# Loading half of the compressed blocks' pages from Pool's queue, with the weights first, and one more step between transposes and state updates

## The chip, the cores and the metric

The kernel runs on one core of a Trainium2 chip. A core has five engines with queues of their own: TensorE (PE: matrix products; PEld is its loading of weights), VectorE (DVE), ScalarE (ACT), GpSimd (POOL) and SyncE (SP), which here only issues transfers. Transfers are issued by SP or by Pool and carried out by 16 DMA engines that both share. The metric is the device time of one execution in microseconds (us); lower is better.

## The reference, cut to what matters

One layer of a hybrid decoder for 1024 prompt tokens and 64 sample tokens (8 sequences of 8 tokens, each with 512 cached tokens in four pages of 128). After one input projection the layer does sparse attention (compressed blocks, selected blocks, sliding window) beside a gated linear recurrence, then a common output projection and an MLP. Two parts matter here.

```
def compress(rows, pe, w1, w2):        # a block of 64 rows -> one compressed key or value
    blk = rows.reshape(b, nc, 64, N_KV_HEADS, 64) + pe
    blk = blk.transpose(...).reshape(b, nc, N_KV_HEADS, 64 * 64)
    return silu(blk @ w1) @ w2         # w1: 4096 x 128, w2: 128 x 64
...
# recurrence, per chunk of 64 tokens and head
S = exp(last) * S + einsum('sd,se->de', k * exp(last - cum), v)
```

`compress` runs over the rows of the prompt and over the cached rows, which lie in 32 pages that a page table names; once for keys (w = 0) and once for values (w = 1).

## The kernel before, in words

The whole layer is one function, `trunk`, written out without loops at run time. Each instruction is put on its engine's queue by a planner: it follows the order in which the Python code issues the instructions as a priority, and takes what its own model of time holds to be ready, so that each queue is a fixed order. A queue is in order: an instruction that waits holds everything behind it.

**Features.** `proj` multiplies the normalised input by 128 columns of the input weights, in three groups of tokens. A group is 24 matmuls (lines 136 to 138, eight blocks of three, since each operand is split in a high and a low half); the generator yields once after 12 of them and once after the evacuation of the group. `weave` alternates such half groups with one step each of a second generator.

**Recurrence.** That second generator is `recurrent`, one for each of four pairs of heads. Its steps are: gate and decay; query; transposes of the weighted keys (L647, L651) and their copies out of PSUM (`k3T`, L648, L649, L652); then, in one step, `swish` of the output gate (L101 on VectorE, L102, L104 and L105 on ScalarE, a product on Pool), the copy of the decay (L657), the first eight state updates (L662) and their copies out of PSUM (L665); a second eight updates; the scan over chunks (L667); attention within a chunk (L678); and so on, to the normalised output in `mix_out`. The updates write the PSUM tile `big`, of which there is one, so the second eight wait for the copies of the first.

**Compression.** After the last pair there is a branch on a flag (L741). Then `compress` issues its loads on SP's queue: 32 pages into the tile `cm` (L263; two runs of 512 bytes in each of 128 partitions, the page number from a register that was read at L732), the position encoding (L267), eight loads of the prompt's rows from `c_d` (L272, runs of 128 bytes), w2 (L275) and three quarters of w1 (L280, 512 KB each, three buffers; the next quarter is loaded when one has been used up). The last two features, 6 and 7, are multiplied while these loads run; then come the 64 products of the compression (L288, two instructions each). From the 45th product on, the first attention scores (`measure`, L843) are put between them. These need the tiles `B1` and `B2`, built by VectorE and ScalarE (L775, L786) from `augk` and `k_d`, which are loaded by SP at L779 and L781; the values (`v_d`, L790) have the same four buffers. The first queries are loaded at L949 and L955 and cast at L958 to L960.

**Pool's queue** before the change: elementwise products, the split of the weights of the recurrent output projection, and ten transfers, among them the writes of `k_d`, `q_d` (L546) and `c_d`, and the mask `dm` (L761).

Of the kernel before, what the change touches and what calls it, by code (L numbers as in the profile page):

```python
# [29 lines left out]
N_PAGES = 32  # L30
POOL_PAGES = 40
# [19 lines left out]
def trunk(ctx: ExitStack, tc: tile.TileContext, I, O):  # L51
# [205 lines left out]
    def compress(ch):  # L257


        mp = pool(ch, "cmp")  # L260
        cm = tl(mp, [128, 2, 161, 32], tag="cm")
        for j in range(N_PAGES):
            S.dma_start(cm[:, :, 4 * j:4 * j + 4].rearrange("p w x s -> p w (x s)"),  # L263
                        I["cache_c"][bass.ds(pages[j], 1)].rearrange("o p (w x) -> (o p) w x", w=2))
            if j % 4 == 3:
                yield -1
        S.dma_start(cm[:, :, 160], I["cmp_pe"])  # L267
        for w in range(2):
            for g in range(2):
                src = c_d[w][g * 64:(g + 1) * 64, :TP].rearrange("d (b h s) -> h d b s", h=2, s=32)  # L270
                for h in range(2):
                    S.dma_start(cm[64 * h:64 * h + 64, w, 128 + g * 16:144 + g * 16], src[h])  # L272
                yield -1
        w2 = tl(mp, [128, 2, 64], tag="w2")
        S.dma_start(w2, I["cmp_w2"])  # L275
        w1 = [[None] * 4 for _ in range(2)]

        def load_w1(w, q):
            w1[w][q] = tl(mp, [128, 8, 128], tag="w1", bufs=3)
            S.dma_start(w1[w][q], I["cmp_w1"][w][:, 8 * q:8 * q + 8])  # L280

        for q in range(3):
            load_w1(0, q)
        yield -2
        for w in range(2):
            ph2 = tl(ps, [128, 512], tag="sc", bufs=SC)
            for s in range(32):
# [59 lines left out]
    with ExitStack() as c:  # L347
# [245 lines left out]
        def recurrent(pr, f, tq, sg):  # L593
# [58 lines left out]
            A.copy(k3T[:64, 8], pt[:64])  # L652
            yield
            swish(sg, tq)

            by_entry = k[:, :TP].rearrange("p (e c) -> p e c", c=16)
            V.tensor_copy(k3[:, :TP].rearrange("p (e c) -> p e c", c=16), decay[:, None, :].to_broadcast([128, 64, 16]))  # L657
            for c0 in range(0, 16, 8):
                pu = tl(ps, [128, 2, 4, 128], tag="big")
                for j in range(8):  # L660
                    ci = c0 + j
                    PE.matmul(pu[:, j % 2, j // 2], k3T[halves[ci % 2], ci // 2], vp[halves[ci % 2], ci // 2],  # L662
                              start=True, stop=True)
                for hs in halves:
                    A.copy(by_entry[hs, :, c0:c0 + 8].rearrange("p e (c u) -> p u c e", u=2), pu[hs, :, :, hs])  # L665
                yield
            V.tensor_tensor_scan(k[:, :TP], k3[:, :TP], k[:, :TP], 0.0, op0=ALU.mult, op1=ALU.add)  # L667
            for hs, copy in zip(halves, (A.copy, V.tensor_copy)):
# [53 lines left out]
        for pr in range(4):  # L722
            f, tq, sg = (tl(hp, [128, T], tag=t) for t in ("tf", "tq", "tg"))
            for j, t in enumerate((f, tq, sg)):
                if j == 2:
                    run(side)
                    side = recurrent(pr, f, tq, sg)
                    next(side)
                weave(scaled(3 * pr + (RF, RQ, RG)[j], t), side if j < 2 else iter(()))
            next(side)  # L730
            if pr == 0:
                pages = [S.value_load(pgt[:1, j:j + 1], min_val=0, max_val=POOL_PAGES - 1) for j in range(N_PAGES)]  # L732
            for i in FEATS[pr]:
                weave(feature(i), side)
        run(side)
# [10 lines left out]
        nl = nlg.rearrange("p t (h r) -> p t r h", r=3)  # L746
        ccp = ExitStack()
        cg = compress(ccp)
        while next(cg) != -2:
            pass  # L750
        for i in FEATS[4]:
            run(feature(i))
        catch_up()
# [22 lines left out]

    for br in range(2):
        ak = tl(bp, [112, TP], tag="b", bufs=4)
        S.dma_start(ak[64:], I["augk"][br])  # L779
        st = tl(bp, [128, TP], tag="b", bufs=4)  # L780
        S.dma_start(st, k_d[br])  # L781
        for g in range(2):
            rows = slice(64 * g, 64 * g + 64)
            for h in range(2):
                bring(B1[64 * h:64 * h + 64, br, g], st[rows])
            V.tensor_tensor(B2[:64, br, g], st[rows], B1[rows, br, g].bitcast(F32), op=ALU.subtract)  # L786
            bring(B2[64:, br, g], ak[64:])
    for t in range(0, 8, 4):
        st = tl(bp, [128, 4, 4, 64], tag="b", bufs=4)
        S.dma_start(st.rearrange("p t b d -> p t (b d)"), v_d[:, t:t + 4])  # L790
        for x in range(4):
            split(st[:, x], VV[:, t + x, :, 0], VV[:, t + x, :, 1])
    cbp.close()
# [343 lines left out]
                          po[64 * g:64 * g + 64].rearrange("p (b c) -> p b c", c=64)[:, :, g * 32 + r * 8:g * 32 + r * 8 + 8])  # L1137
        norm_out(oS, range(4), slice(TP, T), sp, "pt1", 1)

    def out_rnn(rp, groups, other):  # L1140

        units = [(o, n, m) for o, n in groups for m in range(8)]
        stream = ahead([I["w_or"][m] for _, _, m in units], (G,))
# [12 lines left out]
        for u, (o, n, m) in enumerate(units):  # L1156
            wh, wl = next(stream)
            if u == 0:
                yield 0
            if u + 1 < len(units) and units[u + 1][2]:  # L1160
                load(u + 1)
            next(other, None)
            p = tl(ps, [128, 512], tag="mm", bufs=MMB)
            hl = parts[o]
            yield from mm3(p[:, :n], [(wh[:, kc], wl[:, kc], hl[0][:, kc, :n], hl[1][:, kc, :n]) for kc in range(4)])
            if u + 1 < len(units) and not units[u + 1][2]:
                load(u + 1)
            V.tensor_tensor(xs[u][:, :n], xs[u][:, :n], p[:, :n], op=ALU.add)
            S.dma_start(part_d[m][:, o:o + n], xs[u][:, :n])
# [108 lines left out]
    oT0 = H0[:, :4]  # L1278
    rs0 = tl(hp0, [128, n0], tag="rs0")
    crp = ExitStack()  # L1280
    r0 = out_rnn(pool(crp, "outr"), OG, iter(()))
    next(r0)
    attend([(i, g) for g in range(2) for i in range(NQ0)], filler(r0, "outr", "att0", FILL0), oT0, first)

# [214 lines left out]
```

## Time and profile before

| | us |
|---|---|
| median of 3 runs | 1716.74 (1715.77 to 1717.94) |
| the profiled execution's own time | 1714.56 |
| its span in the profile | 1712.8 |

The profile shows one execution. An engine is busy while it works on an instruction; issuing transfers does not count. "<-" in a row of a timeline or of the waits names what ended the idle time before an instruction. The clock (PEclk) is the share of TensorE's full speed that was granted. The DMA share is the mean over 16 engines and can come out above 1.

### The profile page before, as it was taken

Reading aid. Unit: us, or ns where it says so; the run is one execution under the profiler, and the core shown is the slowest. Engines: PE = TensorE matmul, PEld = TensorE weight load, DVE = VectorE, ACT = ScalarE, POOL = GpSimd, SP = SyncE. Lnnn points to the kernel's source line nnn. Section 1 sums busy time; section 2 is a strip of 40 time slices with the busy share of each in tenths; the row PEclk is TensorE's granted clock in tenths of the full one; section 3 lists DMA queues with packets and bytes.
Section 4 is the critical chain, followed back from the end, with each engine's and each line's share of the span. In section 5 each row is a group of like instructions: output and inputs, shape, how many; then the busy total and the mean of one; then the engine's idle time right before and its main releaser. Section 6 shows DMA issues by size and latency. Waiting matters only on the chain.

```text
span 1712.8 us, 25987 instructions
## 1 busy us (share of the span) xinstructions
PE 1636.1 (96%) x9719; PEld 1501.2 (88%) x9741; DVE 947.7 (55%) x1775; ACT 745.3 (44%) x1554; POOL 360.1 (21%) x306
## 2 busy tenths in 40 slices
PE   8999999999599999999999999999999999999999
PEld 6898898988477777788887778999999999999999
DVE  6245655535446778777777756464553352443442
ACT  5334644444336677667766633243421221221211
POOL 0031313211004435333233311010320120120110
PEclk9999999999789999999999999999999999999999
DMA  5333132213934442121211167355322221222222
GB/s 193 121 80 94 54 104 87 65 58 123 247 106 147 138 134 79 40 64 59 70 53 56 53 192 219 115 166 175 108 68 69 74 62 62 81 68 74 62 91 76
DMA packets 135616, 170.84 MB, mean 100 GB/s; under 512 B 37659, under 2 KB 80987, under 8 KB 135483
## 3 DMA queue, kind: packets, MB, share of 16 engines
q1 hardware_dynamic: 134042, 164.38, 31.3%
q0 software_dynamic: 1440, 4.74, 0.9%
q8 instruction: 78, 1.28, 0.3%
q14 instruction: 56, 0.45, 0.1%
HBM read 140.70 MB, written 28.84 MB: 99 GB/s over the span
## 4 chain that ended last, share of the span: by engine, by line
PE 62%; DVE 6%; issue 2%; SPq 2%; ACT 2%; DMA 1%; POOL 0%; DVEq 0%; POOLq 0%; ACTq 0%
PE mm L136 15%; PE mm L137 15%; PE mm L138 15%; PE tr L916 2%; PE O L897 2%; PE O L898 2%; PE sc L843 1%; PE tr L917 1%; PE sc L288 1%; PE sc L844 1%; SPq L263 1%; DVE wl L109 1%; DVE mxs L849 1%; PE sc L1087 1%; PE sc L805 1%
## 5 line engine op out<-in xcount | busy, mean ns | idle before, releaser
L136 PE MATMUL mm<-ah,wh 128*128 128x352 f32 (+1 forms) x736 | 249.1, 338 | 0.0
L136 PE MATMUL mm<-uh,wh 128*128 128x352 f32 (+1 forms) x736 | 244.6, 332 | 0.0
L108 ACT CAST wh<-ws 128x512 fp32r<-128x512 f32 x183 | 105.6, 618 | 313.6 <-PE mm L137 240.0
L137 PE MATMUL mm<-al,wh 128*128 128x352 f32 (+1 forms) x736 | 242.0, 329 | 0.0
L138 PE MATMUL mm<-ah,wl 128*128 128x352 f32 (+1 forms) x736 | 241.4, 328 | 0.0
L138 PE MATMUL mm<-uh,wl 128*128 128x352 f32 (+1 forms) x736 | 240.3, 327 | 0.0
L137 PE MATMUL mm<-ul,wh 128*128 128x352 f32 (+1 forms) x736 | 240.1, 326 | 0.0
L1231 POOL TENSOR_TENSOR sq<-r 128x352 f32<-128x352 f32 (+1 forms) x96 | 99.3, 1034 | 563.4 <-DVE r L1229 553.6
L924 POOL TENSOR_TENSOR pl<-e,ph 128x512 fp32r<-128x512 f32 x88 | 117.8, 1343 | 255.4 <-ACT ph L923 154.0
L136 PE MATMUL mm<-X,wh 128*128 128x364 f32 (+1 forms) x480 | 164.7, 343 | 0.0
L138 PE MATMUL mm<-X,wl 128*128 128x364 f32 (+1 forms) x480 | 160.8, 335 | 3.9 <-PEq L741 3.9
L109 DVE TENSOR_TENSOR wl<-ws,wh 128x512 fp32r<-128x512 f32 x174 | 139.9, 841 | 38.3 <-ACT wh L108 37.8
L137 PE MATMUL mm<-X,wh 128*128 128x364 f32 (+1 forms) x480 | 160.9, 335 | 0.0
L136 PEld LDWEIGHTS mm<-ah,wh 128*128 128x128 f32 x736 | 140.0, 190 | 3.4 <-issue 2.2
L137 PEld LDWEIGHTS mm<-al,wh 128*128 128x128 f32 x736 | 139.5, 190 | 3.9 <-issue 2.7
L136 PEld LDWEIGHTS mm<-uh,wh 128*128 128x128 f32 x736 | 138.9, 189 | 1.9 <-issue 0.8
L138 PEld LDWEIGHTS mm<-uh,wl 128*128 128x128 f32 x736 | 138.2, 188 | 1.5 <-issue 1.2
L137 PEld LDWEIGHTS mm<-ul,wh 128*128 128x128 f32 x736 | 138.4, 188 | 1.1
L138 PEld LDWEIGHTS mm<-ah,wl 128*128 128x128 f32 x736 | 138.9, 189 | 0.5
L1243 DVE TENSOR_TENSOR H<-H,mm 128x352 f32<-128x352 f32 (+1 forms) x92 | 48.8, 530 | 156.2 <-PE mm L138 154.6
L108 ACT CAST wh<-w 128x512 fp32r<-128x512 f32 x153 | 89.5, 616 | 100.3 <-PE mm L137 70.7
L109 DVE TENSOR_TENSOR wl<-w,wh 128x512 fp32r<-128x512 f32 x134 | 115.7, 891 | 28.9 <-ACT wh L108 28.6
(405 smaller groups left out, 3441.3 us busy)
## 6 DMA issues: line engine op xcount, KB each, us to landing
ws<-w_up SPq DMA_DIRECT2D x82, 256.0 KB, 2.8
ws<-w_down SPq DMA_DIRECT2D x80, 256.0 KB, 2.8
w<-w_down SPq DMA_DIRECT2D x48, 256.0 KB, 2.6
w<-w_up SPq DMA_DIRECT2D x46, 256.0 KB, 2.8
w<-w_feat SPq DMA_DIRECT2D x40, 256.0 KB, 2.9
w<-w_or SPq DMA_DIRECT2D x19, 256.0 KB, 2.7
cm<-cache_c SPq DMA_DIRECT2D x32, 128.0 KB, 2.6
w<-cmp_w SPq DMA_DIRECT2D x8, 512.0 KB
```

The source lines that it names most:

```text
L108: A.copy(wh, w)
L109: (eng or V).tensor_tensor(wl, w, wh.bitcast(F32), op=ALU.subtract)
L136: PE.matmul(p, wh, zh, start=i == 0, stop=False)
L137: PE.matmul(p, wh, zl, start=False, stop=False)
L138: PE.matmul(p, wl, zh, start=False, stop=i == n - 1)
L263: S.dma_start(cm[:, :, 4 * j:4 * j + 4].rearrange("p w x s -> p w (x s)"), I["cache_c"][bass.ds(pages[j], 1)].rearrange("o p (w x) -> (o p ...
L897: PE.matmul(po(), vst, ph[:m], start=si == 0, stop=False, skip_group_check=True)
L898: PE.matmul(po(), vst, pl[:m], start=False, stop=end, skip_group_check=True)
L916: PE.matmul(pt, B1[:, br, g, ks], A1, start=True, stop=False)
L924: (G if turn_[0] % 3 < 2 else V).tensor_tensor(pl, e, ph.bitcast(F32), op=ALU.subtract)
L1231: G.tensor_tensor(sq[:, :n], r[:, :n], r[:, :n], op=ALU.mult)
L1243: V.tensor_tensor(H[:, m, sl], H[:, m, sl], p[:, :n], op=ALU.add)
```

## The change: what it does

- `compress`: the first quarter of w1 is issued first. Pages with odd numbers are loaded from Pool's queue, with page numbers that Pool reads itself; pages with even numbers stay on SP. The second quarter comes after the four loads of c_d for the keys, the third after those for the values, and w2 last. The yields between the loads go.
- `recurrent`: one more yield, behind `swish`. Of the two copies of the updated states one goes to VectorE.
- `augk`, `k_d` and `v_d` are loaded from Pool's queue.
- `out_rnn` loses a parameter that was always an empty iterator.

```
@@ -259,29 +259,29 @@

         mp = pool(ch, "cmp")
         cm = tl(mp, [128, 2, 161, 32], tag="cm")
+        w2 = tl(mp, [128, 2, 64], tag="w2")
+        w1 = [[None] * 4 for _ in range(2)]
+
+        def load_w1(w, q):
+            w1[w][q] = tl(mp, [128, 8, 128], tag="w1", bufs=3)
+            S.dma_start(w1[w][q], I["cmp_w1"][w][:, 8 * q:8 * q + 8])
+
+        load_w1(0, 0)
         for j in range(N_PAGES):
-            S.dma_start(cm[:, :, 4 * j:4 * j + 4].rearrange("p w x s -> p w (x s)"),
-                        I["cache_c"][bass.ds(pages[j], 1)].rearrange("o p (w x) -> (o p) w x", w=2))
-            if j % 4 == 3:
-                yield -1
+            eng, page = (G, pages_g[j // 2]) if j % 2 else (S, pages[j])
+            eng.dma_start(cm[:, :, 4 * j:4 * j + 4].rearrange("p w x s -> p w (x s)"),
+                          I["cache_c"][bass.ds(page, 1)].rearrange("o p (w x) -> (o p) w x", w=2))
         S.dma_start(cm[:, :, 160], I["cmp_pe"])
         for w in range(2):
             for g in range(2):
                 src = c_d[w][g * 64:(g + 1) * 64, :TP].rearrange("d (b h s) -> h d b s", h=2, s=32)
                 for h in range(2):
                     S.dma_start(cm[64 * h:64 * h + 64, w, 128 + g * 16:144 + g * 16], src[h])
-                yield -1
-        w2 = tl(mp, [128, 2, 64], tag="w2")
+            if w == 0:
+                load_w1(0, 1)
+        load_w1(0, 2)
         S.dma_start(w2, I["cmp_w2"])
-        w1 = [[None] * 4 for _ in range(2)]
-
-        def load_w1(w, q):
-            w1[w][q] = tl(mp, [128, 8, 128], tag="w1", bufs=3)
-            S.dma_start(w1[w][q], I["cmp_w1"][w][:, 8 * q:8 * q + 8])
-
-        for q in range(3):
-            load_w1(0, q)
-        yield -2
+        yield None
         for w in range(2):
             ph2 = tl(ps, [128, 512], tag="sc", bufs=SC)
             for s in range(32):
@@ -652,6 +652,7 @@
             A.copy(k3T[:64, 8], pt[:64])
             yield
             swish(sg, tq)
+            yield

             by_entry = k[:, :TP].rearrange("p (e c) -> p e c", c=16)
             V.tensor_copy(k3[:, :TP].rearrange("p (e c) -> p e c", c=16), decay[:, None, :].to_broadcast([128, 64, 16]))
@@ -661,8 +662,8 @@
                     ci = c0 + j
                     PE.matmul(pu[:, j % 2, j // 2], k3T[halves[ci % 2], ci // 2], vp[halves[ci % 2], ci // 2],
                               start=True, stop=True)
-                for hs in halves:
-                    A.copy(by_entry[hs, :, c0:c0 + 8].rearrange("p e (c u) -> p u c e", u=2), pu[hs, :, :, hs])
+                for hs, copy in zip(halves, (A.copy, V.tensor_copy)):
+                    copy(by_entry[hs, :, c0:c0 + 8].rearrange("p e (c u) -> p u c e", u=2), pu[hs, :, :, hs])
                 yield
             V.tensor_tensor_scan(k[:, :TP], k3[:, :TP], k[:, :TP], 0.0, op0=ALU.mult, op1=ALU.add)
             for hs, copy in zip(halves, (A.copy, V.tensor_copy)):
@@ -729,7 +730,8 @@
                 weave(scaled(3 * pr + (RF, RQ, RG)[j], t), side if j < 2 else iter(()))
             next(side)
             if pr == 0:
-                pages = [S.value_load(pgt[:1, j:j + 1], min_val=0, max_val=POOL_PAGES - 1) for j in range(N_PAGES)]
+                pages, pages_g = ([eng.value_load(pgt[:1, j:j + 1], min_val=0, max_val=POOL_PAGES - 1) for j in js]
+                                  for eng, js in ((S, range(N_PAGES)), (G, range(1, N_PAGES, 2))))
             for i in FEATS[pr]:
                 weave(feature(i), side)
         run(side)
@@ -746,8 +748,7 @@
         nl = nlg.rearrange("p t (h r) -> p t r h", r=3)
         ccp = ExitStack()
         cg = compress(ccp)
-        while next(cg) != -2:
-            pass
+        next(cg)
         for i in FEATS[4]:
             run(feature(i))
         catch_up()
@@ -776,9 +777,9 @@

     for br in range(2):
         ak = tl(bp, [112, TP], tag="b", bufs=4)
-        S.dma_start(ak[64:], I["augk"][br])
+        G.dma_start(ak[64:], I["augk"][br])
         st = tl(bp, [128, TP], tag="b", bufs=4)
-        S.dma_start(st, k_d[br])
+        G.dma_start(st, k_d[br])
         for g in range(2):
             rows = slice(64 * g, 64 * g + 64)
             for h in range(2):
@@ -787,7 +788,7 @@
             bring(B2[64:, br, g], ak[64:])
     for t in range(0, 8, 4):
         st = tl(bp, [128, 4, 4, 64], tag="b", bufs=4)
-        S.dma_start(st.rearrange("p t b d -> p t (b d)"), v_d[:, t:t + 4])
+        G.dma_start(st.rearrange("p t b d -> p t (b d)"), v_d[:, t:t + 4])
         for x in range(4):
             split(st[:, x], VV[:, t + x, :, 0], VV[:, t + x, :, 1])
     cbp.close()
@@ -1137,7 +1138,7 @@
                           po[64 * g:64 * g + 64].rearrange("p (b c) -> p b c", c=64)[:, :, g * 32 + r * 8:g * 32 + r * 8 + 8])
         norm_out(oS, range(4), slice(TP, T), sp, "pt1", 1)

-    def out_rnn(rp, groups, other):
+    def out_rnn(rp, groups):

         units = [(o, n, m) for o, n in groups for m in range(8)]
         stream = ahead([I["w_or"][m] for _, _, m in units], (G,))
@@ -1159,7 +1160,6 @@
                 yield 0
             if u + 1 < len(units) and units[u + 1][2]:
                 load(u + 1)
-            next(other, None)
             p = tl(ps, [128, 512], tag="mm", bufs=MMB)
             hl = parts[o]
             yield from mm3(p[:, :n], [(wh[:, kc], wl[:, kc], hl[0][:, kc, :n], hl[1][:, kc, :n]) for kc in range(4)])
@@ -1278,7 +1278,7 @@
     oT0 = H0[:, :4]
     rs0 = tl(hp0, [128, n0], tag="rs0")
     crp = ExitStack()
-    r0 = out_rnn(pool(crp, "outr"), OG, iter(()))
+    r0 = out_rnn(pool(crp, "outr"), OG)
     next(r0)
     attend([(i, g) for g in range(2) for i in range(NQ0)], filler(r0, "outr", "att0", FILL0), oT0, first)

```

## Rows read from the trace of the kernel before

**Rows 1.** The page, busy time and share of the span for each engine.
```profile
PE 1636.1 (96%) x9719; PEld 1501.2 (88%) x9741; DVE 947.7 (55%) x1775; ACT 745.3 (44%) x1554; POOL 360.1 (21%) x306
```

**Rows 2.** Waits of TensorE over the span: sum in us, times, longest.
```profile
PE sc L288 <- DMA w<-cmp_w: 18.2, 2, 14.8
PE big L662 <- DVE k3T L649: 8.0, 2, 4.0
PE big L662 <- DVE decay L628: 5.2, 2, 4.0
PE big L662 <- ACT k L665: 1.2, 1, 1.2
```

**Rows 3.** Timeline of TensorE: start and duration in us, instruction, count.
```profile
416.69 0.33 PE L136 MATMUL mm<-X,wh 128*128 128x360 f32 x1
...
420.52 0.33 PE L138 MATMUL mm<-X,wl 128*128 128x360 f32 x1
...
451.35 13.47 PE L288 MATMUL sc<-cm,w 128*128 128x161 f32 x48 [14.78 <-DMA w<-cmp_w]
...
480.46 0.47 PE L843 MATMUL sc<-B,A 128*128 128x128 f32 x1
```

**Rows 4.** Timeline of SP's queue, the loads around the compression.
```profile
410.74 25.73 SPq L263 DMA_DIRECT2D cm<-cache_c  x32
...
437.23 8.56 SPq L272 DMA_DIRECT2D cm<-c_d  x8
...
446.85 1.32 SPq L280 DMA_DIRECT2D w<-cmp_w  x3
...
449.21 0.58 SPq L779 DMA_DIRECT2D b<-augk  x1
...
461.09 0.33 SPq L790 DMA_DIRECT2D b<-v_d  x1
...
463.26 1.92 SPq L280 DMA_DIRECT2D w<-cmp_w  x3
```

**Rows 5.** Busy time by stretch: length, engines, then clock, DMA share, GB/s.
```profile
416.00:436.60 20.60, 19.05 (x111) 18.25 (x110) 10.57 (x20) 10.46 (x22) 3.14 (x3) 1.00 0.66 198
440.00:448.00 8.00, 0.00 (x0) 0.00 (x0) 0.00 (x0) 0.00 (x0) 0.00 (x0) 0.50 1.21 206
```

**Rows 6.** Timeline of pair 1, from the sigmoid to the state copies.
```profile
203.12 1.11 ACT L102 ACTIVATE tq<-tq 128x1088 f32<-128x1088 f32 x1 [4.63 <-DVE tq L101]
...
204.14 0.57 ACT L648 COPY k3T<-big 128x512 f32<-128x512 f32 x1
...
204.74 0.69 DVE L649 COPY k3T<-big 128x512 f32<-128x512 f32 x1 [0.45 <-ACT k3T L648]
...
205.49 2.08 PE L662 MATMUL big<-vp,k3T 64*128 64x128 f32 x16 [3.97 <-DVE decay L628]
...
207.90 2.12 ACT L665 COPY k<-big 64x512 f32<-64x512 f32 x2
```

**Rows 7.** Pool's transfers of q_d: as an instruction, and from issue to landing.
```profile
L546 POOL DMA_DIRECT2D q_d<-nrm x4 | 2.3, 574 | 22.2 <-DVE qS L545 19.5 <-DVE nrm L541 2.7
...
q_d<-nrm POOLq DMA_DIRECT2D x4, 512.0 KB, 4.1
```

**Rows 8.** Timeline of VectorE, the last cast of the first two queries.
```profile
470.78 0.69 DVE L959 TENSOR_TENSOR A<-stage,A 64x512 fp32r<-64x512 f32 x1
```

**Rows 9.** Line 732, the reading of page numbers on SP.
```profile
L732 SPq TENSOR_LOAD <-pgt x32: 262/264/477, 24.2 to 45.8; - x32
```

**Rows 10.** Busy time by stretch behind the updates of pairs 0, 1, 2, 3.
```profile
134.10:141.00 6.90, 5.73 (x52) 5.19 (x53) 2.60 (x2) 5.55 (x8) 2.52 (x1) 1.00 0.01 4
205.50:213.00 7.50, 7.50 (x47) 6.85 (x48) 2.59 (x2) 4.90 (x7) 2.51 (x1) 0.62 0.05 19
278.10:288.00 9.90, 9.81 (x112) 8.95 (x114) 2.14 (x3) 5.73 (x6) 2.50 (x1) 0.83 0.23 70
349.00:357.00 8.00, 8.00 (x51) 7.38 (x52) 0.28 (x1) 4.65 (x6) 2.50 (x1) 0.66 0.03 12
```

More of the change, by code (lines that the diff above doesn't have):

```diff
@@ L261, in compress, with load_w1 @@
         cm = tl(mp, [128, 2, 161, 32], tag="cm")
+        w2 = tl(mp, [128, 2, 64], tag="w2")
+        w1 = [[None] * 4 for _ in range(2)]
+        def load_w1(w, q):
+            w1[w][q] = tl(mp, [128, 8, 128], tag="w1", bufs=3)
+            S.dma_start(w1[w][q], I["cmp_w1"][w][:, 8 * q:8 * q + 8])
+        load_w1(0, 0)
         for j in range(N_PAGES):
[L263 to L266, printed above, removed]
+            eng, page = (G, pages_g[j // 2]) if j % 2 else (S, pages[j])
+            eng.dma_start(cm[:, :, 4 * j:4 * j + 4].rearrange("p w x s -> p w (x s)"),
+                          I["cache_c"][bass.ds(page, 1)].rearrange("o p (w x) -> (o p) w x", w=2))
         S.dma_start(cm[:, :, 160], I["cmp_pe"])
@@ L272, in compress @@
                     S.dma_start(cm[64 * h:64 * h + 64, w, 128 + g * 16:144 + g * 16], src[h])
-                yield -1
-        w2 = tl(mp, [128, 2, 64], tag="w2")
+            if w == 0:
+                load_w1(0, 1)
+        load_w1(0, 2)
         S.dma_start(w2, I["cmp_w2"])
[L276 to L284, printed above, removed]
+        yield None
         for w in range(2):
@@ L654, in recurrent @@
             swish(sg, tq)
+            yield
             by_entry = k[:, :TP].rearrange("p (e c) -> p e c", c=16)
@@ L663, in recurrent @@
                               start=True, stop=True)
-                for hs in halves:
-                    A.copy(by_entry[hs, :, c0:c0 + 8].rearrange("p e (c u) -> p u c e", u=2), pu[hs, :, :, hs])
+                for hs, copy in zip(halves, (A.copy, V.tensor_copy)):
+                    copy(by_entry[hs, :, c0:c0 + 8].rearrange("p e (c u) -> p u c e", u=2), pu[hs, :, :, hs])
                 yield
@@ L731, in trunk @@
             if pr == 0:
-                pages = [S.value_load(pgt[:1, j:j + 1], min_val=0, max_val=POOL_PAGES - 1) for j in range(N_PAGES)]
+                pages, pages_g = ([eng.value_load(pgt[:1, j:j + 1], min_val=0, max_val=POOL_PAGES - 1) for j in js]
+                                  for eng, js in ((S, range(N_PAGES)), (G, range(1, N_PAGES, 2))))
             for i in FEATS[pr]:
@@ L748, in trunk @@
         cg = compress(ccp)
-        while next(cg) != -2:
-            pass
+        next(cg)
         for i in FEATS[4]:
@@ L778, in trunk @@
         ak = tl(bp, [112, TP], tag="b", bufs=4)
-        S.dma_start(ak[64:], I["augk"][br])
+        G.dma_start(ak[64:], I["augk"][br])
         st = tl(bp, [128, TP], tag="b", bufs=4)
-        S.dma_start(st, k_d[br])
+        G.dma_start(st, k_d[br])
         for g in range(2):
@@ L789, in trunk @@
         st = tl(bp, [128, 4, 4, 64], tag="b", bufs=4)
-        S.dma_start(st.rearrange("p t b d -> p t (b d)"), v_d[:, t:t + 4])
+        G.dma_start(st.rearrange("p t b d -> p t (b d)"), v_d[:, t:t + 4])
         for x in range(4):
@@ L1138, in samples, with out_rnn @@
         norm_out(oS, range(4), slice(TP, T), sp, "pt1", 1)
-    def out_rnn(rp, groups, other):
+    def out_rnn(rp, groups):
         units = [(o, n, m) for o, n in groups for m in range(8)]
@@ L1161, in out_rnn @@
                 load(u + 1)
-            next(other, None)
             p = tl(ps, [128, 512], tag="mm", bufs=MMB)
@@ L1280, in trunk @@
     crp = ExitStack()
-    r0 = out_rnn(pool(crp, "outr"), OG, iter(()))
+    r0 = out_rnn(pool(crp, "outr"), OG)
     next(r0)
```

## The prediction

> **What bounds the kernel now.** I read the page first, then the waits of TensorE, then tables of busy time by stretch, and last the timelines of single engines around the two places that the diff touches. The page says that TensorE is busy for 96% of the span [rows 1]. So the span is nearly TensorE's own queue, and a change is worth what it takes out of TensorE's idle time or out of stretches at the lower clock. The list of what TensorE waited for is short, and four of its lines are the two edited places [rows 2]: 18.2 us for the weights of the compression (L288), and 8.0, 5.2 and 1.2 us in front of the state updates (L662).
>
> The first place is the start of the compression. TensorE ends the last feature and has nothing to do until 451.35 us; the wait of 14.8 us is named after the weights, but what was late is the queue ahead of them: SP issues 32 pages from 410.74 on for 25.73 us, then eight loads of c_d for 8.56 us, and only at 446.85 the weights' first quarters [rows 3, 4]. The second wait, 3.4 us after the first 48 instructions (451.35 + 13.47), has the same cause: the next quarters are issued at 463.26, since SP stood behind b<-v_d until 461.09 [rows 3, 4]. The transfers were not the limit while pages were issued: in 416 to 436.6 the DMA engines were 0.66 busy at 198 GB/s [rows 5].
>
> The second place is the chain piece of each head pair. In pair 1 the transposes end, 12 matmuls of a feature follow, and then TensorE stands 3.97 us for the copies of k3T (L648, L649), which ScalarE could not start because it stood 4.63 us in order for L102, the sigmoid of the gate [rows 6]. Pairs 2 and 3 repeat it (4.0 each), pair 0 waits 1.2, and 1.2 again for ScalarE's copy L665 [rows 2].
>
> **The pages and weights, step by step.** SP's queue keeps one weight quarter, 16 pages (half of 25.73, 12.9 us), cmp_pe, eight loads of c_d (8.6) and three small issues. From 410.7 that ends at about 434 instead of 448, ahead of TensorE's last feature at 436.57. Pool takes 16 pages. No row shows Pool issuing a page. The nearest is its write of a 512 KB tile, 0.574 us an issue in the mean of four, landed 4.1 us later [rows 7]; a page has twice as many separate runs (two per partition), so I bound its price by 0.58 and twice that, 1.16, and take 1.16, because SP's own issues grow with the number of runs too (0.80 for a page against 0.44 for a weight quarter, 25.73/32 and 1.32/3, [rows 4]). Then Pool's last page is issued at 411 + 18.6 = 429.9 and lands by 434; with 0.58 nine microseconds earlier. Both ends are before 436.57, so this term costs nothing, and the cover is the two features that run in 410.8 to 436.6.
>
> With both queues issuing, the DMA engines come next. Full, at the rate of [rows 5], they move 300 GB/s. What must land before the first matmul: 4.19 MB of pages (14.0 us), two writes of q_d and two weight quarters (2.1 MB, 7.0 us), four of the eight c_d loads (half of 8.56, 4.3 us, for these were issued against full engines: share 1.21 in 440 to 448 [rows 5]). That is 25.3 us from 411, so 436.3 and a landing. I take 1.5 us of wait at the start; the bounds are nothing and 5 (if the first matmul also waits for the other four c_d loads, 4.3 us).
>
> These 3.4 us go as well: SP no longer stands behind b<-v_d, and a quarter's successor is issued when a quarter has been used, two quarters (about 9 us, 48 instructions in 13.47 us being three quarters [rows 3]) ahead of its use.
>
> The loads of augk, k_d and v_d move to Pool, past dm and the last q_d write, which in this trace end near 440. What is queued behind them on Pool is only the split of output weights, needed much later. They feed B, and B and the queries feed the first attention scores, L843 at 480.46 [rows 3]. Now: first issue 449.21, last cast of the queries done at 471.47 [rows 4, 8], 22.3 us. With an issue between 440 and 443 that gives 462 to 465. TensorE would arrive there 25.7 us of work after its start (480.46 - 451.35 - 3.4), at 436.57 + 1.5 + 25.7 = 463.8. So this is what is late next: 0 to 3 us, taken as 1.
>
> The 16 page numbers read by Pool cost its queue some 0.26 us of load each and as much around it (SP's 32 take 24.2 to 45.8 us, [rows 9]); what hides them is that Pool is busy for 21% of the span [rows 1] and that the numbers are first wanted at 411, so they cost nothing; without that cover it would be 16 times some 0.7, 11 us. The yields and the parameter removed from the generators emit no instruction.
>
> First part: 14.8 + 3.4 - 1.5 - 1 = **15.7 us**, bounds 10 and 18.2.
>
> **The chain piece.** The new yield puts the state updates a half group, 12 matmuls, later in TensorE's order; nothing in front of the updates changes its place, so the copies of k3T are ready when they were. A group of 24 takes 4.0 us (416.69 to 420.52 plus one [rows 3]), so 12 take 2.0. The three waits of 4.0 become 2.0 (6.0 us), pair 0's 1.2 goes (1.2). Everything later in the chain moves back one half group; the chain has 17 steps then, and 18 slots.
>
> The copies of the states are split: ScalarE did two in 2.12 us [rows 6], now one, and VectorE the other. No row has VectorE's copy of this shape; L649, 0.69 us for the same 512 elements per partition [rows 6], is the nearest, and its place behind other steps on VectorE can cost up to a microsecond. I take half of pair 0's second wait as gained, 0.6.
>
> Then the clock. After the 4-us stops the granted clock falls to the lower level: 0.62, 0.83 and 0.66 over 7.5, 9.9 and 8.0 us [rows 10], which is 2.85 + 1.68 + 2.72 = 7.25 us of full-speed time. The stop of 1.2 us in pair 0 was followed by 1.00 [rows 10]. Two microseconds lie between, so I take half. At full clock the second update comes earlier and would meet its copies, about 0.5 us per pair, so half of (7.25 - 1.5) = 2.9.
>
> Second part: 1.2 + 0.6 + 6.0 + 2.9 = **10.7 us**, bounds 4 (clock falls as before, VectorE's copy late) and 16 (no fall, waits gone).
>
> **Rules of the Trainium skill.** The trace shows the engines 0.66 busy under SP's issues, so a second queue can still fill them [rows 5]. Against that, the Trainium skill (DMA: Bandwidth & Descriptors, Issuing engines are not separate DMA queues) says that all queues run on the same 16 DMA engines and that issuing from several saves only the time to issue, usually small; by it the start would stay and the sum would be 3.4 + 10.7 = 14.1, the second rival. By the row the issue time is just what was late, so I keep 26.4.
>
> **The sum.** 15.7 + 10.7 = 26.4 us off the profiled execution's own 1714.56 us (span 1712.8) gives 1688.2. The median of the runs is 2.2 above that execution, so **1690 us**.
>
> **Rivals.**
> 1. The chain piece pays nothing: the wait moves along with the updates, or VectorE's copy stands behind other steps and holds the second update by what the first gained. For it: ScalarE's order is untouched. Against it: the 12 matmuls belong to a feature whose weights are at hand, and they wait for no copy. 1716.7 - 15.7 = 1701.
> 2. The transfers are the limit from the start: the pages, c_d and weights share the engines so that the compression starts where it did, and only the 3.4 us and the second part are gained: 1716.7 - 14.1 = 1702.6. Against it stands the 0.66.
> 3. Something between: the pages of Pool land late by 6 to 8 us (1.6 us a page, or taking turns with SP's), or B is late by as much: 1690 + 7 = 1697.
> 4. The other side: a page costs Pool so much that the compression starts later than now. The start would have to move from 451.35 by the 3.4 + 10.7 us gained elsewhere, to 465.5, so 16 pages from 411 with 4.1 us of landing would have to cost 3.15 us each; at 4 us it starts at 479, and the time is 1730. Against it: four of Pool's issues took 0.574 us on average [rows 7], and VectorE, whatever it might hold up, is busy for only 10.57 of 20.6 us in this stretch [rows 5].
>
> The Trainium skill (SBUF — State Buffer, SBUF: two separate sides) says that VectorE copying float32 within SBUF locks GpSimd out and holds up the descriptors of a DMA issued there; its next section gives 3.1 us for an issue of 0.62 so held. That would be the fourth rival's price almost exactly; no row here shows such a meeting.
>
> 5. The later stages take it back, because the written order of attention and output projection shifts by some steps: 5 us either way, 1712 at worst.
>
> **How the numbers follow.** Forecast 0.60 (its own range 1683 to 1695), rival 1 0.12, rival 2 0.06, rival 3 0.13, rival 4 0.04, rival 5 0.05. About 0.2% (3.4 us) is what a measurement of this kernel can tell from no change. Faster is all but rival 4 and part of 5: 0.92; same 0.04; slower 0.04. The range runs from both upper bounds (34 us, 1682.5) to rivals 1 and 2: 1682 to 1704.
>
> **What the profile after would show.** TensorE's wait at L288 under 3 us in sum, with the compression beginning within 3 us of the last feature. Pool's page issues near 1 us each, all out before the last feature ends. DMA share near 1 in the 25 us of the two features. In front of L662 some 2 us in pairs 1 to 3 and nothing in pair 0, and the clock at 1.00 after at least one of them. A new wait at L843 or L308 of up to 3 us. The prediction is wrong if Pool's issues cost over 1.6 us, if the DMA engines are full and c_d lands after 440, if the updates wait 4 us still, or if the stretch from L843 on gets longer by more than 3 us.

## The result, and the profile after

The changed kernel takes 1694.63 us (median of 4 runs, 1690.34 to 1699.44) against 1716.26 us (4 runs, 1709.82 to 1717.94): a ratio of 0.9882, 95% interval 0.9837 to 0.9926. The forecast was 1690 us in 1682 to 1704. The profiled execution took 1690.45 us with a span of 1688.7, so the profile shows 24.1 us gained where the medians show 21.6: two of the four runs took 1690.4 us, at a mean granted clock of 0.986 and 0.987, and two took 1699 at 0.980.

The page of the changed kernel, busy time of each engine; TensorE has the same share [rows 1] of a shorter span:

```profile
PE 1628.8 (96%) x9719; PEld 1490.9 (88%) x9741; DVE 967.5 (57%) x1783; ACT 735.2 (44%) x1546; POOL 372.9 (22%) x328
```

The waits of TensorE in the changed kernel (sum in us, times, longest), against [rows 2]:

```profile
PE sm L152 <- DVE sql L109: 5.5, 6, 1.2
PE sc L288 <- DMA w<-cmp_w: 4.7, 1, 4.7
...
PE sc L288 <- DMA cm<-c_d: 2.8, 1, 2.8
...
PE big L663 <- DVE k L666: 1.9, 4, 0.6
```

The 18.2 us in front of the compression are 7.5 now, in two other places; the 14.4 us in front of the state updates (L662, now L663) are about 2. Nearly new is the first line, 0.4 us before: matmuls of the chain's norm wait for VectorE.

TensorE's timeline around the compression (start, duration, instruction, count), against [rows 3]:

```profile
428.12 9.09 PE L288 MATMUL sc<-cm,w 128*128 128x161 f32 x32 [2.78 <-DMA cm<-c_d]
441.94 16.31 PE L288 MATMUL sc<-cm,w 128*128 128x161 f32 x58 [4.73 <-DMA w<-cmp_w]
457.85 0.47 PE L844 MATMUL sc<-B,A 128*128 128x128 f32 x1
```

The last feature ends at 428.12 - 2.78 = 425.34 us, 11.2 earlier than at 436.57 (451.35 - 14.78). That is the second part, for up to there no load of the first part has been waited for. The first scores (L844) come at 457.85, 22.6 earlier, and the span ends 24.1 earlier: 12.9 us for the first part, of which 1.5 fall behind the scores. Nothing is given back later.

SP's queue, and then Pool's, over the same stretch; against [rows 4]:

```profile
401.12 15.85 SPq L272 DMA_DIRECT2D cm<-cache_c  x16
...
419.28 5.34 SPq L279 DMA_DIRECT2D cm<-c_d  x4
...
425.42 5.99 SPq L279 DMA_DIRECT2D cm<-c_d  x4
431.45 3.15 SPq L267 DMA_DIRECT2D w<-cmp_w  x1
...
441.96 5.08 SPq L267 DMA_DIRECT2D w<-cmp_w  x3
```

```profile
403.08 5.01 POOL L272 DMA_DIRECT2D cm<-cache_c  x7
...
409.42 2.87 POOL L272 DMA_DIRECT2D cm<-cache_c  x4 [0.25 <-DMA cm<-cache_c]
...
414.38 0.72 POOL L272 DMA_DIRECT2D cm<-cache_c  x1 [1.09 <-DMA cm<-cache_c]
...
428.39 0.52 POOL L780 DMA_DIRECT2D b<-augk  x1
```

SP's 16 pages take 15.85 us, nearly 1 us each where 0.80 was a page's price with one queue; Pool's take about 0.72 each, and Pool stands three times for a transfer of its own pages. Behind the pages SP's loads do not run at the pace of issue either: the third weight quarter of w=0 is issued at 431.45 and takes 3.15 us to get out. What goes with it stands in the table of stretches (length, busy time by engine, then granted clock, DMA share, GB/s), against [rows 5]:

```profile
401.00:414.00 13.00, 13.00 (x71) 13.00 (x70) 4.46 (x9) 4.31 (x10) 11.40 (x16) 0.87 0.97 281
414.00:425.00 11.00, 9.46 (x56) 8.92 (x54) 7.04 (x12) 6.16 (x13) 3.85 (x4) 1.00 0.90 227
425.00:432.00 7.00, 4.22 (x15) 4.00 (x16) 1.70 (x4) 1.01 (x2) 3.29 (x6) 0.52 1.07 227
432.00:442.00 10.00, 5.27 (x20) 3.66 (x19) 0.00 (x0) 6.00 (x6) 0.00 (x0) 0.84 1.10 267
```

Where the DMA engines were 0.66 busy, they are 0.90 to 1.10 busy from 401 to 442 us. The bound has moved from one queue's issue to the transfers.

In the pairs, the timeline of pair 1 (against [rows 6]) and then the clock around the updates of pairs 1 and 2:

```profile
202.56 1.12 ACT L102 ACTIVATE tq<-tq 128x1088 f32<-128x1088 f32 x1 [3.90 <-DVE tq L101]
...
204.18 0.69 DVE L649 COPY k3T<-big 128x512 f32<-128x512 f32 x1 [0.45 <-ACT k3T L648]
...
204.93 1.16 PE L663 MATMUL big<-vp,k3T 64*128 64x128 f32 x16 [0.29 <-DVE decay L628]
```

```profile
198.00:222.00 24.00, 21.60 (x195) 18.69 (x195) 19.07 (x24) 13.91 (x22) 5.99 (x4) 1.00 0.16 47
271.00:294.00 23.00, 22.63 (x212) 20.41 (x210) 16.44 (x20) 9.01 (x10) 5.18 (x4) 1.00 0.39 129
```

The update starts 0.29 us late and not 3.97, and the clock stays at its upper level (1.00, 2.4 GHz; the lower, 1.2 GHz, would be 0.50), in pair 3 too (338 to 360 us). Before, the clock was 0.86, 0.93 and 0.84 over the same three stretches, and 0.62, 0.83 and 0.66 in their lowest parts [rows 10].

### The profile page after: what moved, and what is told of

It is laid out like the page before. It is cut to its first block, busy times and chain, and to the rows that moved or that the text cites. A ratio compares the mean times of both kernels' runs of the same rounds, so it can differ in the third digit from the quotient of the medians.

```text
span 1688.7 us, 26036 instructions
## 1 busy us (share of the span) xinstructions
PE 1628.8 (96%) x9719; PEld 1490.9 (88%) x9741; DVE 967.5 (57%) x1783; ACT 735.2 (44%) x1546; POOL 372.9 (22%) x328
## 4 chain that ended last, share of the span: by engine, by line
PE 61%; DVE 7%; ACT 2%; issue 2%; SPq 2%; DMA 1%; POOL 0%; DVEq 0%; ACTq 0%; POOLq 0%
PE mm L136 15%; PE mm L138 15%; PE mm L137 15%; PE tr L917 2%; PE O L898 2%; PE O L899 2%; PE tr L918 1%; PE sc L844 1%; PE sc L845 1%; DVE wl L109 1%; DVE mxs L850 1%; PE sc L1088 1%; SPq L279 1%; PE sc L806 1%; DMA cm<-cache_c 1%
## 5 line engine op out<-in xcount | busy, mean ns | idle before, releaser
L136 PE MATMUL mm<-X,wh 128*128 128x364 f32 (+1 forms) x480 | 162.1, 338 | 0.0
L137 PE MATMUL mm<-X,wh 128*128 128x364 f32 (+1 forms) x480 | 158.4, 330 | 0.0
L852 ACT ACTIVATE sc<-sc,mxs 128x320 f32<-128x320 f32 (+5 forms) x192 | 100.9, 526 | 64.3 <-DVE mxs L850 62.3
```

What stands on the lines that cost most here:

```text
L136: PE.matmul(p, wh, zh, start=i == 0, stop=False)
L137: PE.matmul(p, wh, zl, start=False, stop=False)
L852: A.activation(sc[:, x], sc[:, x], AF.Exp, bias=mxs[:, br, h, c:c + 1], accum_out=sms[:, br, h, c:c + 1])
```

## The experiments

Each is compared with runs of the kernel before on the same chip; a ratio difference of 0.001 is 1.7 us.

**The chain piece alone.** The kernel before with its two edits (the new yield, and the copies split over ScalarE and VectorE):

```
             swish(sg, tq)
+            yield
...
-                for hs in halves:
-                    A.copy(by_entry[...], pu[hs, :, :, hs])
+                for hs, copy in zip(halves, (A.copy, V.tensor_copy)):
+                    copy(by_entry[...], pu[hs, :, :, hs])
```

> The kernel before with the two edits of the recurrence alone (the yield behind swish, one of the two state copies on VectorE); all loads as before. If the two parts simply add up, the last feature ends some 11 us earlier than before (436.6 to about 425.4), the waits in front of the compression stay at 14.8 and 3.4, and the time is 11 us under before. If the loads' part also helped the recurrence (its registers, the freed SP queue), the gain is under 8 us.

Measured: 1709.82 us, ratio 0.9958 [0.9943, 0.9973], 7.2 us off. So the piece pays, but less than 10.7.

**The yield alone**, without the split:

> The kernel before with the yield behind swish and nothing else. First theory: the yield alone takes the waits at the state updates away, since it moves the end of a pair's output one step back and VectorE so starts the next pair's scan (L610) earlier; the state copy on VectorE gives nothing, because it waits for ScalarE's. Then 11 us or a little more are gained, with new waits of about 1.1 us at L152 in three pairs. Rival: the copy on VectorE frees ScalarE's queue and does half of it; then the yield alone gains only the 12 matmuls' 2 us in four pairs, 7 us, and the clock still falls in pairs 1 to 3.

Measured: 1705.95 us, ratio 0.9937 [0.9916, 0.9957], 10.8 us off. The yield does all of it.

**The split alone**, without the yield:

> The kernel before with one of the two state copies on VectorE and nothing else. First theory (VectorE's copy waits for ScalarE's): no gain, within 1.5 us of before, the 14.4 us of waits in front of the updates stay within 1 us. Rival (ScalarE's queue is what was late): at least 3 us gained, the waits under 11 us.

Measured: 1721.59 us, ratio 1.0019 [1.0001, 1.0037], 3.3 us more. Its waits of TensorE in front of the updates:

```profile
PE big L662 <- DVE k3T L649: 8.0, 2, 4.0
...
PE big L662 <- DVE decay L628: 5.2, 2, 4.0
...
PE big L662 <- DVE k L665: 3.2, 2, 2.3
```

The waits for k3T stay and TensorE waits longer for the copies than the 1.2 us of [rows 2]. The line of the copies in this kernel says why (duration minimum, median, maximum; then what VectorE and ScalarE stood for):

```profile
L665 ACT COPY k<-big x8: 1035/1042/1051, 136.5 to 358.4; 64x512 f32<-64x512 f32 x8
L665 DVE COPY k<-big x8: 1015/1042/1059, 138.7 to 359.5; 64x512 f32<-64x512 f32 x8
...
  ACT k L665: 18.4, 6
```

VectorE's copy is no shorter than ScalarE's, and six times VectorE stands, 18.4 us in sum, until ScalarE's copy ends. Two copies one after the other take as long as before, and now hold two engines.

**The loads alone**: the changed kernel without yield and split.

> The changed kernel without the two edits of the recurrence: pages split over two queues, weights first, augk, k_d and v_d from Pool. If the parts add up: 13 us under before, compression 2 to 3 us behind the last feature, and a second wait of 4 to 5 us for the third quarter of w1. If the transfers had been the limit already: 3.4 us under before.

Measured: 1702.59 us, ratio 0.9921 [0.9893, 0.9949], 13.6 us off. The parts multiply: 0.9958 x 0.9921 = 0.9879 for the change as it is (0.9882 measured).

**The changed kernel without the split**, both copies on ScalarE:

> The changed kernel with one edit undone: both copies of each state update are on ScalarE again. First theory, the two copies never run side by side and VectorE's only waits behind ScalarE's: 2 to 4 us under the changed kernel (about 1691 by the difference of 3.8 us between the two runs of the chain piece with and without the split), and the idle time of VectorE behind ScalarE's copy of k gone. Rival, the transfers set the end from 401 us on and take back what the pairs give: the last feature ends 2 to 4 us earlier, the waits of the matmuls at L288 grow by as much, and the time stays that of the changed kernel.

Measured: 1692.22 us, ratio 0.9858 [0.9834, 0.9883]; 0.9937 x 0.9921 is 0.9858 too. It is the fastest version measured. By itself the step from 0.9882 lies within the intervals, and in the two profiles the last feature ends alike (425.77 us without the split, 425.34 with it). But three comparisons (yield and split against yield alone, split alone against before, and this one) put the split at 3.6, 3.3 and 4.1 us of cost.

**The third weight quarter issued earlier** in the changed kernel:

```
             if w == 0:
                 load_w1(0, 1)
-        load_w1(0, 2)
+                load_w1(0, 2)
```

> The changed kernel with the third weight quarter issued on SP ahead of the second four loads of c_d, not behind them. First theory, the order on SP sets when the third quarter lands: the wait of 4.7 us in front of the 58 matmuls at L288 goes, and 3 to 5 us of it come off the time. Rival, the DMA engines are full from 401 to 457 us and only the order of the same bytes changes: the wait moves to a later quarter or to the loads of c_d behind it, and the time stays within 1 us of the changed kernel.

Measured: 1696.0 us, ratio 0.9872 [0.9848, 0.9895]: no measurable change. TensorE's timeline:

```profile
428.97 13.49 PE L288 MATMUL sc<-cm,w 128*128 128x161 f32 x48 [2.59 <-DMA w<-cmp_w]
448.10 11.87 PE L288 MATMUL sc<-cm,w 128*128 128x161 f32 x42 [5.64 <-DMA w<-cmp_w]
```

The third quarter is there, so 48 instructions run without a stop, and then the fourth is late by 5.64 us: the wait has moved by one quarter, as the rival says.

**All pages on SP** in the changed kernel (`eng, page = S, pages[j]`):

> The changed kernel with all 32 page loads on SP again, the weights' order and the rest as changed. First theory, one queue's issue time paces the pages: SP takes some 26 us for them as before, against 15.9 us, so the first matmul at L288 starts 8 to 10 us later than at 428.1 us and the time rises by 7 to 10 us. Rival, the transfers themselves are the limit and one queue fills the DMA engines as well as two: the pages' share of the DMA engines stays near .9 to 1.1 and the time rises by less than 3 us.

Measured: 1707.74 us, ratio 0.9947 [0.9929, 0.9965], 11 us over the changed kernel. SP's queue, then the stretches in which it issues the pages:

```profile
403.36 25.39 SPq L272 DMA_DIRECT2D cm<-cache_c  x32
```

```profile
401.00:414.00 13.00, 11.51 (x60) 11.54 (x61) 5.08 (x10) 4.21 (x9) 1.88 (x2) 0.87 0.64 195
414.00:425.00 11.00, 11.00 (x67) 10.77 (x65) 4.77 (x10) 4.24 (x10) 0.58 (x1) 1.00 0.71 211
```

One queue leaves the engines at 0.64 to 0.71, as in [rows 5]. The split of the pages over two queues is most of the first part.

**VectorE copying while Pool issues.** Extra work, 24 copies that nobody reads, ahead of the loads:

```
+        scr = tl(mp, [128, 2, 1024], tag="scr")
+        V.memset(scr[:, 0], 0.0)
+        for _ in range(24):
+            V.tensor_copy(scr[:, 1], scr[:, 0])
         load_w1(0, 0)
```

> The changed kernel with 24 copies of 1024 floats from SBUF to SBUF on VectorE (and one memset) put ahead of the page loads in program order, so that VectorE copies while Pool issues its 16 pages; this work is extra and its results are not used. First theory, Pool's issue of a page does not depend on what VectorE does: 0.7 to 0.8 us each as in the changed kernel, and the time rises by the VectorE work that is in the way, at most some 20 us. Rival, the fourth of the prediction: Pool's issues stretch while VectorE copies, to 3 us each or more.

Measured: 1708.69 us in one run, the extra work being in the way. Pool's pages, and the copies (duration minimum, median, maximum):

```profile
L276 POOL DMA_DIRECT2D cm<-cache_c x16: 720/772/1107, 402.7 to 416.4; - x16
```

```profile
L272 DVE COPY scr<-scr x24: 677/683/2391, 404.0 to 432.5; 128x1024 f32<-128x1024 f32 x24
```

VectorE was busy for 12.54 of the 14.5 us in which Pool issued, 7.72 of them with these copies. A page costs Pool 0.72 to 1.11 us there against 0.71 to 0.78 in the changed kernel: a touch, and nowhere 3. The longest copy, 2.39 us for one of 0.68, met a subtraction of 1.30 us on Pool (416.66 to 419.05 us, Pool's from 417.19 to 418.49).

**B's loads on SP again** in the changed kernel (augk, k_d and v_d issued by `S`):

> The changed kernel with the loads of augk, k_d and v_d for B on SP again, the rest as changed. First theory, the DMA engines are full from 401 to 457 us, so the two early loads of k_d and augk take 1.4 MB out of the transfers that L288 waits for; without them the two waits at L288 (7.5 us in sum) fall by 3 to 5 us, but B is built later and the first scores wait for VectorE, as SP issues these loads some 10 us later: the time stays within 3 us of the changed kernel. Rival, Pool's early issue of B is worth what SP's place in line cost: the first scores wait 5 us or more for B and the time rises by as much.

Measured: 1702.43 us, ratio 0.9911 [0.9893, 0.9929], 5 us over the changed kernel, though the intervals overlap. TensorE's timeline:

```profile
429.15 9.11 PE L288 MATMUL sc<-cm,w 128*128 128x161 f32 x32 [0.50 <-issue]
439.59 4.64 PE L288 MATMUL sc<-cm,w 128*128 128x161 f32 x16 [1.33 <-DMA w<-cmp_w]
456.95 10.22 PE L288 MATMUL sc<-cm,w 128*128 128x161 f32 x36 [12.73 <-DMA w<-cmp_w]
```

With 1.4 MB fewer under way the third quarter is there at 439.59 us and not at 441.94, issued at 431.08 and 431.45: the early loads of B do take the transfers' time from the compression. The first wait, 0.50 and not 2.78, says nothing of them: the last feature ended 3.3 us later here (428.65), and in the changed kernel B's first load is issued at 428.39, behind the first matmul at 428.12. But SP now issues the fourth quarter behind B's loads, and 12.73 us are waited for it. The first theory had the mechanism right, at 2.4 us in place of 3 to 5, and overlooked the place in SP's queue.

**Pages in halves.** Without the split copies; each page loaded as two halves, those of w=0 first and on both queues, those of w=1 on SP; four weight buffers:

```
+        for w in range(2):
             for j in range(N_PAGES):
+                eng, page = (G, pages_g[j // 2]) if j % 2 and w == 0 else (S, pages[j])
+                eng.dma_start(cm[:, w, 4 * j:4 * j + 4]...)
             ... c_d of w; if w == 0: load_w1(0, 1), (0, 2), (0, 3)
```

> The changed kernel with both copies of a state update on ScalarE, every page loaded as two halves (the half for w=0 on SP and Pool by turns, first; the half for w=1 all on SP, behind the weights of w=0), and four weight buffers in place of three. First theory, the bytes that the matmuls of w=0 need are 4.7 MB of the 7.3 MB before them now, so at 260 GB/s they have landed before the last feature ends: both waits at L288 in w=0 go, the first scores come 3 to 7 us earlier than at 457.9 us and the time falls by as much against the run with both copies on ScalarE. Rival, the first scores then wait for B, which VectorE ends at 456 us and cannot build earlier: the gain is under 1.5 us. A second rival: a page in two halves costs SP and Pool more issue time than it saves, and the waits at L288 stay 7 us in sum.

Measured: 1702.17 us, ratio 0.9906 [0.9892, 0.9919], 8 us over the version without the split. TensorE's timeline, and VectorE's:

```profile
424.82 17.80 PE L288 MATMUL sc<-cm,w 128*128 128x161 f32 x64 [0.45 <-DMA cm<-cache_c]
455.57 0.58 PE L308 MATMUL mm<-hg,w 128*64 128x64 f32 x4 [12.95 <-DMA w<-cmp_w]
```

```profile
442.71 0.16 DVE L293 COPY bcol<-sc 128x1 f32<-128x1 f32 x1 [8.81 <-PE sc L288]
...
443.48 1.40 DVE L776 CAST B<-b 64x1024 fp32r<-64x1024 f32 x2
...
454.96 0.32 DVE L298 TENSOR_TENSOR hid<-hid,sg 128x160 f32<-128x160 f32 x1
```

The transfers no longer hold the keys' half: 64 instructions run from the end of the last feature without a stop. Then TensorE stands 12.95 us at L308. The row names w2, but its load was issued at 445.53 and landed 3.2 us later; what is late is hg, whose product (L298) stands in VectorE's order behind the building of B and of the split values, 443.48 to 454.96. So the rival on VectorE was right, with another place and a higher price.

**The same, with hsel and anyv loaded from Pool**:

> As the kernel with halved pages, with the small loads of hsel and anyv issued from Pool and not behind SP's queue. First theory, VectorE stands in front of B's copies because its multiplication by anyv waits for that load: B is built up to 6 us earlier and the first scores follow, 1 to 5 us under the kernel with halved pages alone. Rival, B waits for its own bytes (k_d lands 8.7 us after its issue) or the scores do not wait for B: no change within 1 us.

Measured: 1699.72 us, ratio 0.9900 [0.9883, 0.9916], no measurable change from the run before. VectorE multiplies by anyv at 430.94 us and still builds B behind L293, which waits for the compression's matmuls; TensorE's wait at L308, named after hg here, is 13.4 us. The order on VectorE, not that load, holds B.

**Weights first, pages whole.** Without the split copies; four weight buffers, `load_w1(0, 1)` to `(0, 3)` ahead of c_d of w=1, hsel and anyv on Pool:

> The changed kernel with both copies of a state update on ScalarE, four weight buffers, all weight quarters of w=0 issued ahead of the second four loads of c_d, and hsel and anyv loaded from Pool; pages whole and on both queues. First theory, the DMA engines have some room left (share .84 to .90 in 442 to 452 us) and what is needed first now comes first: of the 7.5 us of waits at L288 some 3 us stay, the first scores come at about 455 us and the time is 2 to 3 us under the run with both copies on ScalarE. Rival, the engines are full: the sum of the waits at L288 stays 6 to 8 us, and the time is that of the run with both copies on ScalarE within 1.5 us. A second rival, what now comes later (c_d of w=1, stage) is late itself and stops VectorE or the matmuls of w=1: the time rises by 3 us or more.

Measured: 1699.41 us, ratio 0.9895 [0.9873, 0.9918], 6 us over the version without the split, with intervals that overlap. The waits at L288 fall to 3.9 us and the first scores come at 455.99, 1.9 us before those of the changed kernel, as the first theory has it. The loss is behind them, at the clock (third column from the right); first this kernel, then the changed one:

```profile
470.00:485.00 15.00, 11.77 (x60) 9.82 (x60) 6.43 (x35) 5.09 (x22) 0.00 (x0) 0.56 0.37 110
485.00:500.00 15.00, 15.00 (x58) 11.04 (x57) 9.08 (x27) 7.98 (x24) 1.26 (x1) 0.64 0.15 44
```

```profile
470.00:485.00 15.00, 14.53 (x78) 10.46 (x77) 7.56 (x32) 5.59 (x19) 1.27 (x1) 0.77 0.37 113
485.00:500.00 15.00, 13.95 (x75) 11.03 (x75) 13.62 (x38) 10.88 (x32) 3.49 (x3) 1.00 0.40 116
```

In 30 us TensorE has 0.56 and 0.64 of its clock against 0.77 and 1.00 (the version without the split has 0.77 and 1.00 too), 8.6 us of full-speed time. It was busy for 11.77 of the 15 us in which the clock was low first; at its start TensorE waits 0.9 us for `hg` (L303, at 470.06 us), 0.4 (470.95) and 1.4 for `kc` (L318, 472.80), where the changed kernel's wait for `hg` is 0.2. That the loss is this stretch is read from one profile of each, and that these waits brought the clock down is not shown.

## Why the prediction was right, and which steps were not

**The bound and the two places** were right. Apart from the new wait at L152 no other line of TensorE's waits moved by more than 1.2 us, and the two parts add up in the runs (0.9958 x 0.9921).

**The pages.** The page price on Pool, taken as 1.16 us from the bounds 0.58 and 1.16, is 0.72; either would have served. (16 pages at 1.16 from 411 end at 429.6, not at 429.9, which changes nothing.) The 0.66 meant what the prediction read in it: with the pages on one queue again the engines fall back to 0.64 and 0.71 and 11 us are lost. The Trainium skill (DMA: Bandwidth & Descriptors, Issuing engines are not separate DMA queues) says that a second issuing engine saves only issue time, usually small. The first half holds here; the second does not, for the issue time it saved was what set the end. What the rule warns of came next: the engines are 0.90 to 1.10 busy from 401 to 442 us.

**The start of the compression** was to wait 1.5 us and waits 2.78: 12.0 us gained, 13.3 expected. The sum of bytes and rate that gave 1.5 was good to 1.3 us, in part by luck: from 401 to 428.1 us the engines moved 251 GB/s and not 300, and the 4.3 us that the sum set apart for c_d made up for it.

**The step that failed in the first part** is "these 3.4 us go as well". They became 4.73. The step looked at SP's queue, where nothing stands in front of the weights any more, and left out what the step before it had found, that the DMA engines would be full: a quarter issued at 431.45 behind c_d, and beside k_d and augk from Pool, lands at 441.9. The run with the earlier issue shows that the order on SP does not mend it, the run with B's loads on SP that fewer bytes under way do in part (the quarter is there 2.4 us earlier). At L288 the trace has 7.5 us in sum where less than 3 was forecast. B late by 1 us, the other doubtful term, did not show: no wait of TensorE for B stands in front of L844.

**The chain piece** gave 11.2 us in the profile and 10.7 was forecast, which is luck: the make-up is another, and the runs give 7.2. In four other profiles of kernels with yield and split (the chain piece alone, the earlier quarter, all pages on SP, B's loads on SP) the last feature ends at 428.3, 426.4, 427.5 and 428.7 us, not at 425.3. The yield was to turn three waits of 4.0 into 2.0, on the ground that nothing in front of the updates changes its place. The update waits are nearly gone. In pair 1 the transposes start 1.1 us later (199.49 against 198.37), since the norm's matmuls L152 now wait for VectorE, and the update starts 0.56 earlier: VectorE runs the next pair's scan (L610, 2.60 us) ahead of the norm's last steps, at 179.45 and not 182.28, so that ScalarE gets to its sigmoid at 202.56 and not 203.12, and 24 feature matmuls, not 12, lie between. The price is the 5.5 us at L152. The clock, of which half was counted, is kept whole in this profile; in those four it was 0.93 over 198 to 222 us. By the runs the yield alone is worth 10.8 us.

**The step that failed in the second part** is the split of the copies, forecast at a gain of 0.6 and, by the runs without the change of the loads, worth a loss of 3 to 4. The forecast took the 0.69 us of L649 for VectorE's copy and its place behind other steps for the risk. Both numbers missed what stands in the same row: "[0.45 <-ACT k3T L648]" [rows 6]. L649 reads the same PSUM tile as L648 and starts when that one ends, and the copies at L666 are programmed alike, with a wait of VectorE for ScalarE's semaphore:

```profile
L666 ACT COPY k<-big x8: 1027/1041/1060, 136.3 to 347.6; 64x512 f32<-64x512 f32 x8
L666 DVE COPY k<-big x8: 1029/1033/1058, 138.6 to 348.6; 64x512 f32<-64x512 f32 x8
...
  ACT k L666: 8.8, 6
```

So the second half never ran beside the first, and at 1.03 us it is no faster. Common tiles alone do not order two engines: in the next step of each pair both copy the halves of one SBUF tile, k, into one other tile, side by side (pair 0; VectorE's timeline, then ScalarE's).

```profile
145.66 1.07 DVE L670 COPY states<-k 64x1024 f32<-64x1024 f32 x1
```

```profile
145.71 2.02 ACT L670 COPY states<-k 64x1024 f32<-64x1024 f32 x1 [3.48 <-DVE k L668]
```

What L649 and L666 have and L670 has not is a source in PSUM. The Trainium skill (PSUM — Partial Sum Buffer, PSUM bank collisions raise a hardware error) asks that two engines be kept apart in one bank only where they touch the same quarter of the partitions; these two copies read different halves. By that the wait is the program's and not the chip's. No run here took it away.

Some of the split's price goes with the clock. Over 198 to 222 us it was 1.00 in all five profiles of kernels with the yield and without the split, and 0.93 in five of the six with both; the sixth is the changed kernel's own. What stopped TensorE there was not taken apart.

**The rivals.** Rival 1 falls with the yield's 10.8 us. Rival 2 has its mechanism, full engines, but not its place: the start still came 23.2 us earlier, 12.0 of them by the loads. What rival 3 saw late in the pages was late in the weights. Rival 4's trap, VectorE holding up Pool's issue, was tried: 1.11 us at the worst, against the 3.15 it needed, with VectorE busy for 12.54 of 14.5 us, 7.72 of them with such copies. (The 0.62 and 3.1 us that the prediction sets beside this rival belong, in its source, to a whole transfer and not to its issue alone.) With Pool's arithmetic it is another matter (last section). Rival 5 did not happen: from the first scores on the changed kernel takes 1230.9 us against 1232.3.

**Why 1694.6 and not 1690.** By the runs the first part is 13.6 us in place of 15.7 and the second 7.2 in place of 10.7. The first shortfall is the weight quarter, less than the interval of that run can tell; the second is the split.

## What to carry to other kernels

When one queue's issue is the bound and the DMA engines are partly idle, a second queue pays at once, but cost everything behind it against full engines: a load that was late by its place in line is then late by bytes. Issuing one load earlier only moved the wait here, and the orders that shortened it lost more behind it. Before work is shared between two engines, read in the trace whether two engines have ever run side by side out of that tile; a releaser in brackets beside the nearest row is the warning. And when one early wait is taken out of a kernel whose order is fixed, look at the next engine's order (VectorE's, here) before spending more on the first.

## What the hardware showed that was not expected

VectorE can stand still in the middle of its work while Pool calculates. In the changed kernel a subtraction on VectorE took 2.13 us beside an operation of 2.52 us on Pool, and ended 0.40 us after it, where one with Pool idle takes 0.53 (at 419.62). In the kernel before, the same subtraction took 2.06 us beside 2.51 on Pool (208.03 and 207.18) and ended 0.40 after it too. VectorE's and then Pool's timeline:

```profile
207.47 2.13 DVE L109 TENSOR_TENSOR sql<-sq,sqh 128x364 fp32r<-128x364 f32 x1
```

```profile
206.68 2.52 POOL L157 TENSOR_TENSOR tg<-tg,tq 128x1088 f32<-128x1088 f32 x1 [7.15 <-ACT tq L105]
```

The Trainium skill (SBUF — State Buffer, Who interferes with whom) has the rule: an instruction of VectorE with two inputs in SBUF contends with one of Pool that reads SBUF. These rows agree. The section counts copies in a two-port mode among them too, and the copy of 2.39 us in the experiment above fits that. Beside such copies an issue of a page on Pool took at most 1.11 us, where 0.72 is its median in the changed kernel.
